# One forget-bias tile per head, held for a whole head pair

## The chip, the core and the metric

The kernel runs on one core of a Trainium2 chip. The metric is the device time of one execution in microseconds (us), as the median of several runs. Beside it there is one profiled execution: its instructions on five engines (PE is TensorE, DVE VectorE, ACT ScalarE, POOL GpSimd, SP SyncE, which here only issues DMAs), its DMA packets and the clock that TensorE was granted.

## What is computed

One layer of a streaming encoder, for a prompt of 1040 positions (16 meta tokens and 1024 frames) and a sample group of 32 positions with a cache of 272. One projection makes the queries, keys and values of two attention groups and a gate. The first group (4 heads, "differential") has a bias from the distance of query and key. The second (8 heads, "forgetting") has a bias that is a difference of running sums of log forget gates:

```
F = jnp.cumsum(LF, axis=1)
...
sf = jnp.einsum('bqhe,bkhe->bhqk', qf, Kf).astype(f32) * scale
sf = sf + (Fq_t[:, :, :, None] - Fk_t[:, :, None, :])
sf = jnp.where(kidx[None, :] <= qidx[:, None], sf, NEG)
pf = jax.nn.softmax(sf, axis=-1)
of = jnp.einsum('bhqk,bkhe->bqhe', pf.astype(Vf.dtype), Vf)
...
y = x + (out.astype(x.dtype) * jax.nn.silu(gate)) @ w_out_l
```

A term that is the same for all keys of a query falls out of the softmax. So the kernel needs, of `Fq - Fk`, only the part that runs over the keys, against any reference column.

## The kernel before

The work is cut into tasks, some thousand of them, each with an engine, a cost, a priority, dependencies and the buffers that it takes and gives back. A planner (`Graph.order`) walks through them in modelled time and writes out, for each engine, the order in which its instructions stand. The order is fixed when the program is built: on the chip each engine and the SP queue goes through its list in order, and waits on semaphores for its operands. So a task with another cost, another dependency or another buffer can move instructions on every engine behind it.

There are eight head pairs, `p` 0 to 7. Pairs 0 to 3 are the four differential heads, pairs 4 to 7 hold two forgetting heads each. A pair has its projections of v, k and q (line 827), its sample part, and its attention units. In a forgetting pair there are eight units, head by query group: `units = [(h, gg) for gg in range(4) for h in range(2)]` (line 1846). A query group has 256 queries, which are two blocks `i` of 128; block `i` attends to 144 + 128 i keys.

A block of a forgetting head goes through this chain: two matmuls a chunk of up to 512 keys into a score buffer `sc` and one that adds the mask (lines 1235 and 1237); a fused DVE pass that adds the bias tile `G`, scales and takes the minimum (line 1249); the exponential on ACT (1255); the reciprocal on DVE (1259); a split into two halves of 16 bits on ACT, POOL or DVE (1290 to 1323); a DMA transpose by SP (1335); and the products with the values on PE (1351, 1352, 1354), called the value products below. The planner places matmuls of projections (line 827, of later pairs or of the gate) between the scores of a block and its value products, and PE goes through them while the chain runs on the other engines.

The bias tile of a forgetting head comes to its unit in this way. `forget_tasks` has the running sum `F` of eight heads on eight partitions. Four DVE passes (line 1113) subtract, one for each query group, the value at the first query of the group, and four DMAs store the rows in the DRAM tensor `G_s` (line 1115). Before a pair begins, its 2 heads by 4 groups are loaded as eight rows (1177), multiplied by a scale of the pair on POOL (1180) and stored to `G_t` (1184). Then each unit has one DMA that spreads its row over 128 partitions (1192), as wide as the keys of its group: 272, 528, 784 or 1040 columns. The tile is one of the ring "G", which has two buffers (`RINGS`, line 247), so that a unit's tile can be fetched when the unit before the last one has read its own. The ring also serves the distance tile of the differential pairs and the two norm weights.

After the last pair the output projection (line 1770) runs by blocks of 128 rows, each of which needs the mixed values (`mix_s`) of all pairs and the gates (`gate_s`).

Of the kernel before, what the change touches and what calls it, by code (L numbers as in the profile page):

```python
# [9 lines left out]
F32 = mybir.dt.float32  # L10
# [4 lines left out]
ALU = mybir.AluOpType  # L15
# [6 lines left out]
NH = 8  # L22
# [67 lines left out]
class Graph:  # L90
# [9 lines left out]
    def add(self, eng, cost, fn, prio, deps=(), acq=(), use=(), move=0.0, spare=()):  # L100
        t = Task(eng, cost, fn, prio, deps, acq, use, move, spare)
        t.seq = len(self.tasks)
        self.tasks.append(t)
        return t
# [125 lines left out]
def tile_hymba(  # L230
# [72 lines left out]

    mix_s = dr.tile([1024, 1056], F32, tag="mix_s", name="mix_s")
    gate_s = dr.tile([1024, NT], F32, tag="gate_s", name="gate_s")
    G_s = dr.tile([NH, 4 * 1040], F32, tag="G_s", name="G_s")
    G_t = dr.tile([NH, 4 * 1040], F32, tag="G_t", name="G_t")
    Gs_s = dr.tile([NH, LS], F32, tag="Gs_s", name="Gs_s")
    mix_v = mix_s.rearrange("(k p) c -> p k c", p=128)
    gate_v = gate_s.rearrange("(k p) c -> p k c", p=128)  # L310
# [35 lines left out]
    def A(h, n, rows=128):  # L346
        assert h.ring == "arena" and n <= h.size
        return arena[:rows, h.at:h.at + n]
# [630 lines left out]
    def forget_tasks(prio):  # L979
# [123 lines left out]
                                          scalar1=F[:, c - 1:c], scalar2=None, op0=ALU.add)  # L1103
            carry = [add("dve", 800, fa, prio, [tm] + carry, [Fh] if part == 0 else [], [ph] + ([Fh] if part else []))]
        G_done = {}
        for gg in range(4):
            n = 1040
            gh = Hold("arena", n)

            def fg(gg=gg, n=n, gh=gh):  # L1110
                F = A(Fh, 1040, NH)
                b = 16 + 256 * gg
                dve.tensor_scalar(out=A(gh, n, NH), in0=F[:, :n], scalar1=F[:, b:b + 1], scalar2=None, op0=ALU.subtract)
            tg = add("dve", 65 + 0.6 * n, fg, prio, carry, [gh], [Fh])
            G_done[gg] = dma(lambda gg=gg, n=n, gh=gh: sp.dma_start(
                out=G_s[:, 1040 * gg:1040 * gg + n], in_=A(gh, n, NH)), prio, [tg], [], [gh])

        ph, FSh, GSh = Hold("pj"), Hold("arena", LS), Hold("arena", LS)

# [25 lines left out]
        w = -(-nk // n // 16) * 16  # L1145
        return [(i * w, min(nk, (i + 1) * w)) for i in range(n)]

    def bias_tasks(p, hd, gg, prio, G_done):

        h = Hold("G")  # L1150
        loc = {}
        if p < 4:
            sl = 2.0 ** (-2 * (p + 1))
            eh = Hold("arena", 1040)

            def f1():
                E = A(eh, 1040)
                pool.iota(E, pattern=[[-1, 1040]], base=912, channel_multiplier=1, allow_small_or_imprecise_dtypes=True)
                pool.tensor_scalar(out=E, in0=E, scalar1=Q[p]["inv"], scalar2=sl, op0=ALU.mult, op1=ALU.mult)

            def f2():
                E = A(eh, 1040)
                D = T([128, 1040], F32, "G", RINGS["G"])
                dve.scalar_tensor_tensor(out=D, in0=E, scalar=-1.0, in1=E, op0=ALU.mult, op1=ALU.max)
                loc["t"] = D
            t1 = add("pool", 2500, f1, prio, [cn.get("bias"), cn["gate"], Q[p]["t_tau"]], [eh, h], spare=[1088, 1088])
            t2 = add("dve", c_dve(1040), f2, prio, [t1], [], [eh, h])
            t3 = add("pool", 250, lambda: pool.memset(loc["t"][0:64, 976:1040], BIG), prio, [t2], [], [h])
            cn["bias"] = t3
            return loc, h, t3  # L1170
        n = 272 + 256 * gg
        if ("G", p) not in samp:
            gh = Hold("arena", 1040)
            a = 2 * (p - 4)

            def fl():
                sp.dma_start(out=A(gh, 1040, 8), in_=G_s[a:a + 2].rearrange("h (g n) -> (h g) n", g=4))

            def fm():
                pool.tensor_scalar(out=A(gh, 1040, 8), in0=A(gh, 1040, 8), scalar1=Q[p]["inv"][:8], scalar2=1.0,  # L1180
                                   op0=ALU.mult, op1=ALU.mult)

            def fo():
                sp.dma_start(out=G_t[a:a + 2].rearrange("h (g n) -> (h g) n", g=4), in_=A(gh, 1040, 8))
            t = dma(fl, prio - 50, [G_done[x] for x in range(4)] + [Q[p]["t_tau"]], [gh], kb=33)
            t = add("pool", 100 + 1.1 * 1040, fm, prio - 50, [t], [], [gh])
            samp["G", p] = dma(fo, prio - 50, [t], [], [gh], kb=33)

        def f():
            loc["t"] = T([128, 1040], F32, "G", RINGS["G"])  # L1190
            c = 1040 * (4 * hd + gg)
            sp.dma_start(out=loc["t"][:, :n], in_=G_t.rearrange("h n -> (h n)")[None, 8320 * (p - 4) + c:8320 * (p - 4) + c + n]
                         .broadcast_to([128, n]))
        cn["bias"] = dma(f, prio, [samp["G", p], cn["bias"]], [h], kb=n / 2)
        return loc, h, cn["bias"]

    mix_done = {}
# [645 lines left out]
    def pair_tasks(p):  # L1843
        base = 1000 + 100 * p
        sample_tasks(p, base + 3, G_done)
        units = [(0, gg) for gg in range(4)] if p < 4 else [(h, gg) for gg in range(4) for h in range(2)]
        av = {}
        dist = None
        for u, (hd, gg) in enumerate(units):
            if p >= 4 or u == 0:  # L1850
                dist = bias_tasks(p, hd, gg, base + u - 1, G_done)
            if hd == 0:
                av = {}
            unit_tasks(p, hd, gg, base + u, dist, av)

    done = -1
    for idx, (kind, p) in enumerate(order):
# [56 lines left out]
```

## Time and profile before

| what | us |
|---|---|
| median of 3 runs (881.67 to 883.38) | 882.83 |
| the profiled execution | 879.12 |
| its span | 877.4 |
| PE busy | 703.1 (80%) |
| DVE busy | 633.0 (72%) |
| ACT busy | 496.5 (57%) |
| POOL busy | 414.3 (47%) |
| packets of the DMA queue of SP, as a share of 16 engines | 60.4% |

The span is what the trace covers; the rest of the profiled execution's time lies around it. A busy time is a sum over stages with different limits, so that the table alone doesn't tell what a change is worth. In the order of time the stages are: the norm and the first projections with the forget gates (to about 134 us), mostly differential pairs (to about 420), the forgetting pairs (to about 740), the output projection (to the end).

### The profile page before, as it was taken

Reading aid. Unit: us, or ns where it says so; the run is one execution under the profiler, and the core shown is the slowest. Engines: PE = TensorE matmul, PEld = TensorE weight load, DVE = VectorE, ACT = ScalarE, POOL = GpSimd, SP = SyncE. Lnnn points to the kernel's source line nnn. Section 1 sums busy time; section 2 is a strip of 40 time slices with the busy share of each in tenths; the row PEclk is TensorE's granted clock in tenths of the full one; section 3 lists DMA queues with packets and bytes.
Section 4 is the critical chain, followed back from the end, with each engine's and each line's share of the span. In section 5 each row is a group of like instructions: output and inputs, shape, how many; then the busy total and the mean of one; then the engine's idle time right before and its main releaser. Section 6 shows DMA issues by size and latency. Waiting matters only on the chain. (4 is left out here: it accounts for less than half of the span.)

```text
span 877.4 us, 14974 instructions
## 1 busy us (share of the span) xinstructions
PE 703.1 (80%) x4967; PEld 456.3 (52%) x4967; DVE 633.0 (72%) x1672; ACT 496.5 (57%) x1136; POOL 414.3 (47%) x602
## 2 busy tenths in 40 slices
PE   4578887987876999899796978689788962888776
PEld 4455554665544576566564755356556542233333
DVE  5976587877766887988985857497797895454443
ACT  5843574666553776676675665377568752242222
POOL 2575233977556866866743654445452244200000
PEclk7679989999998999999998989799999985698899
DMA  8672426454423554554499688467959989753511
GB/s 248 122 147 62 93 54 88 106 94 103 95 65 74 127 102 98 115 117 115 105 194 182 127 168 163 111 144 167 208 123 204 277 204 243 232 173 121 153 63 49
DMA packets 240558, 119.27 MB, mean 136 GB/s; under 512 B 150569, under 2 KB 229745, under 8 KB 240481
## 3 DMA queue, kind: packets, MB, share of 16 engines
q1 hardware_dynamic: 240480, 118.32, 60.4%
q8 instruction: 39, 0.64, 0.3%
q14 instruction: 39, 0.31, 0.1%
HBM read 57.18 MB, written 22.07 MB: 90 GB/s over the span
## 5 line engine op out<-in xcount | busy, mean ns | idle before, releaser
L827 PE MATMUL pj<-hT,Whi 128*128 128x384 f16 (+4 forms) x1328 | 314.7, 321 | 2.0 <-DVE ge L938 1.5
L827 PE MATMUL pj<-hT,Wlo 128*128 128x416 f16 (+4 forms) x664 | 212.6, 320 | 4.4 <-DVE Wlo L648 4.4
L827 PEld LDWEIGHTS <-Whi 128*128 128x128 f16 x1328 | 133.3, 102 | 78.5 <-issue 11.5
L1249 DVE CUSTOM_DVE_ANT_0 arena<-sc,G,stats 128x400 f32<-128x400 f32 (+6 forms) x224 | 129.9, 590 | 43.3 <-PE sc L1235 22.4
L1255 ACT ACTIVATE arena<-arena,stats 128x144 f32<-128x144 f32 (+7 forms) x128 | 99.9, 780 | 38.8 <-DVE stats L1249 31.6
L1235 PE MATMUL sc<-k,q 128*128 128x400 f16 (+6 forms) x448 | 97.1, 317 | 29.4 <-DVE stats L1249 25.7
L583 POOL TENSOR_SCALAR diag<-ident,stats 128x128 bf16<-128x128 f32 x51 | 26.1, 513 | 154.9 <-ACT Wlo L1737 68.5
L827 PEld LDWEIGHTS <-Wlo 128*128 128x128 f16 x664 | 67.6, 102 | 38.1 <-DVE Wlo L648 4.7
L1351 PE MATMUL av<-arena,vn 128*128 128x128 f16 x288 | 43.9, 236 | 45.2 <-DMA arena<-arena 44.7
L1235 PEld LDWEIGHTS <-q 128*128 128x128 f16 x448 | 40.8, 101 | 57.6 <-issue 41.1
L627 ACT ACTIVATE Wlo<-raw 128x1024 bf16<-128x1024 f32 x27 | 28.5, 1055 | 63.8 <-DMA raw<-in_w_in_dram 63.8
L1770 PEld LDWEIGHTS <-Whi 128*128 128x128 f16 (+2 forms) x304 | 30.1, 102 | 58.7 <-issue 16.5
L827 PE MATMUL pj<-hT,Wghi 128*128 128x256 f16 (+2 forms) x240 | 58.2, 326 | 0.0
L1770 PE MATMUL pj<-arena,Whi 128*128 128x512 f16 (+4 forms) x152 | 49.7, 413 | 9.8 <-ACT Whi L1740 7.1
L1352 PEld LDWEIGHTS <-vn 128*128 128x128 f16 x288 | 30.7, 107 | 48.6 <-issue 47.6
L1290 POOL TENSOR_TENSOR arena<-arena 128x16 f16<-128x16 f32 (+7 forms) x56 | 46.5, 853 | 12.4 <-ACT arena L1284 12.1
L1306 DVE SCALAR_TENSOR_TENSOR arena<-arena,stats 128x128 f16<-128x128 f32 (+4 forms) x80 | 49.6, 663 | 2.6 <-ACT arena L1298 2.4
L1323 POOL TENSOR_TENSOR arena<-arena 128x16 f16<-128x16 f32 (+3 forms) x48 | 36.0, 773 | 25.8 <-ACT arena L1317 25.7
L1789 ACT ACTIVATE arena<-arena 128x512 bf16<-128x512 f32 (+3 forms) x19 | 11.5, 603 | 61.4 <-DVE arena L1784 61.4
L1352 PE MATMUL av<-arena,vn 128*128 128x128 f16 x288 | 44.3, 237 | 0.0
L1784 DVE SCALAR_TENSOR_TENSOR arena<-pj,stats,arena 128x512 f32<-128x512 f32 (+3 forms) x19 | 13.7, 721 | 42.3 <-PE pj L1770 38.9
L587 PE MATMUL tr<-diag,onesb 128*128 128x128 bf16 x51 | 11.7, 229 | 36.9 <-POOL diag L583 24.6
(310 smaller groups left out, 1786.7 us busy)
## 6 DMA issues: line engine op xcount, KB each, us to landing
raw<-in_w_in_dram SPq DMA_DIRECT2D x32, 512.0 KB, 7.5
arena<-in_x_prompt_dram SPq DMA_DIRECT2D x16, 512.0 KB, 9.7
raw<-in_w_out_dram SPq DMA_DIRECT2D x16, 512.0 KB, 4.6
k<-k SPq DMA_DIRECT2D x16, 268.0 KB, 3.4
G<-G_t SPq DMA_DIRECT2D x8, 520.0 KB, 4.7
mix_s<-mx SPq DMA_DIRECT2D x32, 128.0 KB, 3.4
arena<-mix_s SPq DMA_DIRECT2D x8, 512.0 KB, 6.3
arena<-gate_s SPq DMA_DIRECT2D x8, 512.0 KB, 6.0
```

The costliest lines, as they stand in the source:

```text
L583: pool.tensor_scalar(out=loc["d"], in0=ident, scalar1=col_, scalar2=1.0, op0=ALU.mult, op1=ALU.mult)
L627: ta = add("act", c_act(1024), lambda: act.activation(out=loc["lo"].bitcast(BF16), in_=loc["raw"], func=AF.Abs, accum_out=a), prio, [tl], ...
L827: mm(out, (W["hi"], W["hi"], W["lo"])[w][:, k, :], (hTh, hTl, hTh)[w][:, k, c0:c1], start=i == 0, stop=i == 23)
L1235: mm(s[:, :b - a], q, K[p]["t"][:, m, x, a:b], start=x == 0, stop=x == 1 and not mask)
L1249: dve.tensor_tensor_reduce(out=A(ph, nk)[:, a:b], in0=loc["s"][:, :b - a], in1=bl["t"][:, o + a:o + b], scale=Q[p]["tau"], scalar=3e38 if ...
L1255: te = add("act", c_act(nk) + 150, lambda ph=ph, nk=nk, mn=mn, sm=sm: act.activation(out=A(ph, nk), in_=A(ph, nk), func=AF.Exp, scale=-1.0 ...
L1290: (pool if on_pool else dve).tensor_tensor(out=A16(w, o, o + b - a), in0=x[:, a:b], in1=A16(w, h, h + b - a), op=ALU.subtract)
L1306: dve.scalar_tensor_tensor(out=A16(w, o, o + b - a), in0=x[:, a:b], scalar=rk, in1=A16(w, h, h + b - a), op0=ALU.mult, op1=ALU.subtract)
L1323: pool.tensor_tensor(out=A16(w, o, o + b - a), in0=x[:, a:b], in1=A16(w, h, h + b - a), op=ALU.subtract)
L1351: mm(out, vn[:, j, 128 * hd:128 * hd + 128], hi, start=j == 0, stop=False)
L1352: mm(out, vn[:, j, 128 * hd:128 * hd + 128], lw, start=False, stop=False)
L1770: mm(d, a, b, start=k == 0 and i == 0, stop=k == 7 and i == len(ops) - 1)
```

## The change

The bias of a forgetting head is made once for all four query groups. One DVE pass subtracts the value of `F` at column 528 in place of four that subtract the value at the first query of a group; one store in place of four fills `G_s`; the scale of a pair is applied to two rows in place of eight; and one broadcast of 1040 columns for each head takes the place of four of 272, 528, 784 and 1040. `pair_tasks` asks for a head's tile at its first unit (priorities `base - 1` and `base`) and hands the same tile to all four units, so that a pair holds both buffers of the ring until its heads are through.

```diff
--- before.py
+++ after.py
@@ -303,8 +303,8 @@
 
     mix_s = dr.tile([1024, 1056], F32, tag="mix_s", name="mix_s")
     gate_s = dr.tile([1024, NT], F32, tag="gate_s", name="gate_s")
-    G_s = dr.tile([NH, 4 * 1040], F32, tag="G_s", name="G_s")
-    G_t = dr.tile([NH, 4 * 1040], F32, tag="G_t", name="G_t")
+    G_s = dr.tile([NH, 1040], F32, tag="G_s", name="G_s")
+    G_t = dr.tile([NH, 1040], F32, tag="G_t", name="G_t")
     Gs_s = dr.tile([NH, LS], F32, tag="Gs_s", name="Gs_s")
     mix_v = mix_s.rearrange("(k p) c -> p k c", p=128)
     gate_v = gate_s.rearrange("(k p) c -> p k c", p=128)
@@ -1103,17 +1103,14 @@
                                           scalar1=F[:, c - 1:c], scalar2=None, op0=ALU.add)
             carry = [add("dve", 800, fa, prio, [tm] + carry, [Fh] if part == 0 else [], [ph] + ([Fh] if part else []))]
         G_done = {}
-        for gg in range(4):
-            n = 1040
-            gh = Hold("arena", n)
-
-            def fg(gg=gg, n=n, gh=gh):
-                F = A(Fh, 1040, NH)
-                b = 16 + 256 * gg
-                dve.tensor_scalar(out=A(gh, n, NH), in0=F[:, :n], scalar1=F[:, b:b + 1], scalar2=None, op0=ALU.subtract)
-            tg = add("dve", 65 + 0.6 * n, fg, prio, carry, [gh], [Fh])
-            G_done[gg] = dma(lambda gg=gg, n=n, gh=gh: sp.dma_start(
-                out=G_s[:, 1040 * gg:1040 * gg + n], in_=A(gh, n, NH)), prio, [tg], [], [gh])
+
+        gh = Hold("arena", 1040)
+
+        def fg():
+            F = A(Fh, 1040, NH)
+            dve.tensor_scalar(out=A(gh, 1040, NH), in0=F, scalar1=F[:, 528:529], scalar2=None, op0=ALU.subtract)
+        tg = add("dve", 65 + 0.6 * 1040, fg, prio, carry, [gh], [Fh])
+        G_done["p"] = dma(lambda: sp.dma_start(out=G_s, in_=A(gh, 1040, NH)), prio, [tg], [], [gh])
 
         ph, FSh, GSh = Hold("pj"), Hold("arena", LS), Hold("arena", LS)
 
@@ -1145,7 +1142,7 @@
         w = -(-nk // n // 16) * 16
         return [(i * w, min(nk, (i + 1) * w)) for i in range(n)]
 
-    def bias_tasks(p, hd, gg, prio, G_done):
+    def bias_tasks(p, hd, prio, G_done):
 
         h = Hold("G")
         loc = {}
@@ -1168,30 +1165,28 @@
             t3 = add("pool", 250, lambda: pool.memset(loc["t"][0:64, 976:1040], BIG), prio, [t2], [], [h])
             cn["bias"] = t3
             return loc, h, t3
-        n = 272 + 256 * gg
-        if ("G", p) not in samp:
+        if hd == 0:
             gh = Hold("arena", 1040)
             a = 2 * (p - 4)
 
             def fl():
-                sp.dma_start(out=A(gh, 1040, 8), in_=G_s[a:a + 2].rearrange("h (g n) -> (h g) n", g=4))
+                sp.dma_start(out=A(gh, 1040, 2), in_=G_s[a:a + 2])
 
             def fm():
-                pool.tensor_scalar(out=A(gh, 1040, 8), in0=A(gh, 1040, 8), scalar1=Q[p]["inv"][:8], scalar2=1.0,
+                pool.tensor_scalar(out=A(gh, 1040, 2), in0=A(gh, 1040, 2), scalar1=Q[p]["inv"][:2], scalar2=1.0,
                                    op0=ALU.mult, op1=ALU.mult)
 
             def fo():
-                sp.dma_start(out=G_t[a:a + 2].rearrange("h (g n) -> (h g) n", g=4), in_=A(gh, 1040, 8))
-            t = dma(fl, prio - 50, [G_done[x] for x in range(4)] + [Q[p]["t_tau"]], [gh], kb=33)
+                sp.dma_start(out=G_t[a:a + 2], in_=A(gh, 1040, 2))
+            t = dma(fl, prio - 50, [G_done["p"], Q[p]["t_tau"]], [gh], kb=8)
             t = add("pool", 100 + 1.1 * 1040, fm, prio - 50, [t], [], [gh])
-            samp["G", p] = dma(fo, prio - 50, [t], [], [gh], kb=33)
+            samp["G", p] = dma(fo, prio - 50, [t], [], [gh], kb=8)
+        c = 2 * (p - 4) + hd
 
         def f():
             loc["t"] = T([128, 1040], F32, "G", RINGS["G"])
-            c = 1040 * (4 * hd + gg)
-            sp.dma_start(out=loc["t"][:, :n], in_=G_t.rearrange("h n -> (h n)")[None, 8320 * (p - 4) + c:8320 * (p - 4) + c + n]
-                         .broadcast_to([128, n]))
-        cn["bias"] = dma(f, prio, [samp["G", p], cn["bias"]], [h], kb=n / 2)
+            sp.dma_start(out=loc["t"], in_=G_t[c:c + 1].broadcast_to([128, 1040]))
+        cn["bias"] = dma(f, prio, [samp["G", p], cn["bias"]], [h], kb=520)
         return loc, h, cn["bias"]
 
     mix_done = {}
@@ -1845,13 +1840,13 @@
         sample_tasks(p, base + 3, G_done)
         units = [(0, gg) for gg in range(4)] if p < 4 else [(h, gg) for gg in range(4) for h in range(2)]
         av = {}
-        dist = None
+        dist = {}
         for u, (hd, gg) in enumerate(units):
-            if p >= 4 or u == 0:
-                dist = bias_tasks(p, hd, gg, base + u - 1, G_done)
+            if hd not in dist:
+                dist[hd] = bias_tasks(p, hd, base + u - 1, G_done)
             if hd == 0:
                 av = {}
-            unit_tasks(p, hd, gg, base + u, dist, av)
+            unit_tasks(p, hd, gg, base + u, dist[hd], av)
 
     done = -1
     for idx, (kind, p) in enumerate(order):
```

The line numbers of the changed kernel are smaller by five from `bias_tasks` on: 1187 and below there answer to 1192 here. The planner's order moves on all five engines, from the forget gates on. Three places follow.

The first is the SP queue where pair 6 ends and pair 7 begins (`G<-G_t` is the spreading of a bias tile, `arena<-arena` the transpose of a block with 2 i + 3 tiles of 128, `raw` a weight load, `stg` rows of new keys on their way out, `ckr` and `cvr` cached keys and values). Before:

```order
L1192 DMA G<-G_t 128x272
L1335 DMA_TRANSPOSE arena<-arena 128x15x128
L793 DMA vm<-vm 16x256
L625 DMA raw<-in_w_in_dram 128x8x128
L1373 DMA mix_s<-mx 128x256
L1335 DMA_TRANSPOSE arena<-arena 128x17x128
L1192 DMA G<-G_t 128x272
L1457 DMA ckr<-in_cache_fox_k_dram 128x2x128
L1458 DMA ckr<-in_cache_fox_k_dram 16x128
L1192 DMA G<-G_t 128x528
L945 DMA gate_s<-ge 128x384
L1335 DMA_TRANSPOSE arena<-arena 128x15x128
```

The changed kernel, at the same place:

```order
L1188 DMA G<-G_t 128x1040
L1368 DMA mix_s<-mx 128x256
L1330 DMA_TRANSPOSE arena<-arena 128x15x128
L793 DMA vm<-vm 16x256
L625 DMA raw<-in_w_in_dram 128x8x128
L1330 DMA_TRANSPOSE arena<-arena 128x17x128
L1188 DMA G<-G_t 128x1040
L718 DMA out_dram<-stg 128x2x128
L721 DMA out_dram<-stg 16x128
L1330 DMA_TRANSPOSE arena<-arena 128x15x128
L1330 DMA_TRANSPOSE arena<-arena 128x17x128
```

The first broadcasts of a pair stand where they stood, among the transposes of the last blocks of the pair before, but are 1040 columns wide in place of 272; the later ones of 528, 784 and 1040 are gone from the list.

The second is PE near the end of pair 7, behind the scores of the largest block of head 0 (`q_7799` and `q_7754` are its queries, `vn` values, `Whi` and `Wlo` gate weights). Before:

```order
L1235 MATMUL sc<-k,q_7799 128x336
L1237 LDWEIGHTS identb
L1237 MATMUL sc<-mkb,identb 128x128
L1351 LDWEIGHTS vn
L1351 MATMUL av<-arena,vn 128x128
L1352 LDWEIGHTS vn
L1352 MATMUL av<-arena,vn 128x128
```

The changed kernel:

```order
L1230 MATMUL sc<-k,q_7754 128x336
L1232 LDWEIGHTS identb
L1232 MATMUL sc<-mkb,identb 128x128
L827 LDWEIGHTS Whi
L827 MATMUL pj<-hT,Whi 128x416
L827 LDWEIGHTS Wlo
L827 MATMUL pj<-hT,Wlo 128x416
L827 LDWEIGHTS Whi
L827 MATMUL pj<-hT,Whi 128x416
```

Matmuls of the gate projection, which were all used up before this point, now stand between these scores and the next value products: 32 of them lie between the scores of this block and its own value products, where there were none.

The third is no excerpt but a count over both lists. Between the last score matmul of a forgetting block and its value products there stood on average 126.6 matmuls on PE, and now 134.6; blocks with fewer than 45 projection matmuls in between were 14 of 64, and are 9 of 64. Single blocks move both ways: head 1, block 4 of pair 4 goes from 40 to 55, the same block of pair 5 from 39 to 47, head 0, block 6 of pair 6 from 120 to 88.

## Rows read from the trace of the kernel before

**Rows 1.** Windows by stage: stretch, PE, PEld, DVE, ACT, POOL busy, granted clock, DMA, GB/s
```profile
371.00:705.00 334.00, 280.33 (x2257) 195.63 (x2256) 258.20 (x741) 221.37 (x514) 163.71 (x265) 0.95 0.76 161
...
420.00:740.00 320.00, 253.34 (x2032) 177.32 (x2030) 242.03 (x689) 202.88 (x461) 146.84 (x229) 0.92 0.82 175
```

**Rows 2.** Waits of PE, 420 to 719 us: us in total, times, longest
```profile
PE av L1351 <- DMA arena<-arena: 33.5, 17, 8.7
PE sc L1235 <- DVE stats L1249: 10.9, 13, 3.0
```

**Rows 3.** Timeline of PE: start, us, operation, idle before and its releaser
```profile
440.02 0.34 PE L827 MATMUL pj<-hT,Whi 128*128 128x416 f16 x1
440.19 0.34 PE L827 MATMUL pj<-hT,Wlo 128*128 128x416 f16 x1
...
448.47 0.22 PE L1351 MATMUL av<-arena,vn 128*128 128x128 f16 x1 [1.33 <-DMA arena<-arena]
...
479.36 0.27 PE L1351 MATMUL av<-arena,vn 128*128 128x128 f16 x1 [6.62 <-DMA arena<-arena]
...
559.91 0.27 PE L1351 MATMUL av<-arena,vn 128*128 128x128 f16 x1 [8.72 <-DMA arena<-arena]
...
660.00 0.22 PE L1351 MATMUL av<-arena,vn 128*128 128x128 f16 x1 [4.34 <-DMA arena<-arena]
...
682.17 0.22 PE L1351 MATMUL av<-arena,vn 128*128 128x128 f16 x1 [0.32 <-DMA arena<-arena]
682.23 0.22 PE L1352 MATMUL av<-arena,vn 128*128 128x128 f16 x1
```

**Rows 4.** Timeline of the SP queue: start, us, what it issued
```profile
440.61 0.32 SPq L1192 DMA_DIRECT2D G<-G_t  x1
...
442.65 2.04 SPq L1335 DMA_TRANSPOSE arena<-arena  x1
...
466.75 0.53 SPq L1192 DMA_DIRECT2D G<-G_t  x1
467.33 0.63 SPq L625 DMA_DIRECT2D raw<-in_w_in_dram  x1
468.15 10.00 SPq L1335 DMA_TRANSPOSE arena<-arena  x2
...
677.42 0.52 SPq L1192 DMA_DIRECT2D G<-G_t  x1
678.11 1.20 SPq L1335 DMA_TRANSPOSE arena<-arena  x1
```

**Rows 5.** DMA queue of SP, and bias broadcasts by size: KB each, us to landing
```profile
q1 hardware_dynamic: 240480, 118.32, 60.4%
...
G<-G_t SPq DMA_DIRECT2D x8, 520.0 KB, 4.7
...
G<-G_t SPq DMA_DIRECT2D x8, 392.0 KB, 4.3
...
G<-G_t SPq DMA_DIRECT2D x8, 264.0 KB, 6.2
...
G<-G_t SPq DMA_DIRECT2D x8, 136.0 KB, 3.4
```

**Rows 6.** Line 1249, the reader of the bias: what its engine waited for
```profile
  PE sc L1235: 22.4, 20
  PE sc L1237: 13.3, 15
  DMA gs<-Gs_s: 1.6, 1
```

**Rows 7.** Lines 1192 and 1113: durations in ns, min, median, max
```profile
L1192 SPq DMA_DIRECT2D G<-G_t x32: 319/392/1590, 371.0 to 701.4; - x32
...
L1113 DVE TENSOR_SCALAR arena<-arena x4: 743/744/749, 133.7 to 135.7; 8x1040 f32<-8x1040 f32 x4
```

**Rows 8.** Waits of the SP queue: us in total, times, longest
```profile
SPq L1192 <- DVE stats L1249: 9.5, 9, 4.1
```

**Rows 9.** Second broadcast of pair 7 (SP) and its first reader (DVE), from timelines
```profile
658.47 0.38 SPq L1192 DMA_DIRECT2D G<-G_t  x1
...
663.59 0.37 DVE L1249 CUSTOM_DVE_ANT_0 arena<-sc,G,stats 128x144 f32<-128x144 f32 x1 [4.32 <-PE sc L1237]
```

**Rows 10.** The chain that ended last, in order of time
```profile
718.22 0.50 DVE arena L1249
...
731.20 5.05 DMA arena<-arena
...
746.87 9.96 PE pj L1770 x24
```

## The prediction

> **What bounds the kernel now.** I read the page by stages first. No engine is full in the stage that the change touches: from 420 to 740 us PE is busy for 253 of 320 us and DVE for 242, while the DMA engines have their highest share of any stage, 0.82 [rows 1]. So the next view is who PE waits for there. Nearly all of it is one kind: from 420 us to the last scores (719 us) PE stands at the first value product of a block and waits 33.5 us, in 17 waits, for the DMA transpose of the same block; the next kind, scores that wait for a free score buffer, has 10.9 us [rows 2]. The timeline shows the waits one by one, the longest at 559.91 and 479.36 us [rows 3]. The SP queue at the second of them shows why a transpose is late: a bias broadcast and a weight load go out at 466.75 and 467.33, and the two transposes behind them hold the queue for 10.00 us [rows 4].
>
> The chain that ended last goes from the last scores (the DVE pass at 718.22) over one transpose of 5.05 us into the output projection [rows 10], and everything behind is the same work in both kernels. The last scores come after the same PE work in both orders. So what the change is worth is what it does to the waits of PE before 719 us.
>
> The bias tile itself is not waited for: of the time that DVE stood before line 1249, all was for scores or other things, none for a `G` from `G_t` [rows 6]. The broadcasts matter through what they do to the DMA engines, to the SP queue and to the planner's order.
>
> **Part A, traffic.** The 32 broadcasts move 8 x (520 + 392 + 264 + 136) = 10,496 KB, the new eight 8 x 520 = 4,160 KB [rows 5]. That is 6,336 KB or 6.49 MB less. All packets of the queue took 60.4% of 877.4 us for 118.32 MB [rows 5], which is 530 us or 4.48 us for a MB, so the change takes away some 29 us of all 16 engines, out of 0.76 x 334 = 254 us that they are busy from 371 to 705 us [rows 1]: 11%.
> Most of this lies beside other work. Of the 17 waits, eight have a bias broadcast issued shortly before or during the flight of their transpose; the first is at 448.47 (broadcast at 440.61, transpose at 442.65), the last at 682.17 (677.42 and 678.11) [rows 3, 4]. Together they last 11.8 us. A broadcast can have cost a wait no more than its own time, 0.52 x 4.48 = 2.3 us for the widest, which cuts the 6.62 us at 479.36 to 2.3 and leaves 7.5 us as the upper end. The lower end is a loss, since the first two broadcasts of each pair grow by 384 KB, 1.7 us of all engines each, among the transposes of the largest blocks; that is the second rival below. I take a gain of 3 us, nearer to nothing than to the upper end, because the longest wait, 8.72 us, has no broadcast of the bias ahead of it.
> The trace prices a MB at 4.48 us in a mix that is mostly short packets. The Trainium skill gives the SBUF side of the DMA engines a ceiling of 435 GB/s (DMA: Bandwidth & Descriptors, Specifications). By that figure alone the traffic taken away would be an estimated 15 us, not 29, the most that the widest broadcast could have cost 1.2 us, and this part would be worth 2 us in place of 3. No row here shows a broadcast at that rate.
>
> **Part B, order.** The count at the end of the part on the change says that a block has on average 8 more matmuls between its scores and its value products. Their starts lie 0.17 us apart where they are 416 columns wide and 0.06 where they are value products [rows 3], so 8 of a mix are about 1 us of more cover. Taking at most 1 us from each of the 17 waits gives 13.6 us, which would be all if order did nothing else. It does: head 1, block 4 of pair 4, the one that waits 6.62 us, gains 15 projection matmuls (2.6 us), the same block of pair 5, with 8.72 us, gains 8 (1.4 us), but head 0, block 6 of pair 6, with 4.34 us at 660.00, loses 32 (5.4 us) [rows 3]. The planner puts value products where it believes that they are ready, so a longer cover also says that it sees the chain on DVE, ACT and POOL as longer. The ends are a gain of 26 us (all 33.5 us but what part A has taken) and a loss of 9 us (one more wait like the longest). I take 4 us, a third of the 13.6.
>
> **Part C, issue and DVE.** SP has 24 broadcasts less of 0.39 us, 9.4 us of queue in over 330, and it stood 9.5 us in nine waits for a tile that DVE had not given back [rows 7, 8]; with a tile that is held, six of eight such waits per pair fall away. Nothing but a transpose behind them makes that count, and those are in part A. Three DVE passes of 0.744 us go, at 133.7 to 136.4 us [rows 7]; nobody waits for them directly, and PE has projections there. The ends are 0 and 2.2 us, and I take 1, since DVE is what gives score and projection buffers back. The scale on POOL has as many instructions as before, on two partitions in place of eight.
>
> **Sum.** 3 + 4 + 1 = 8 us. From the profiled execution's 879.1 us this gives 871; the median of the runs lies 3.7 us above that execution, so the forecast for the median is 882.8 - 8 = **874.8 us**, 0.9% faster.
>
> **Rivals.** *Hidden anyway.* No engine waits for the bias, the transfers were fetched one unit ahead, and the waits of PE would form again at other blocks, since the planner aims its value products at the same readiness as before. For it speaks that nothing on DVE waited for `G_t` [rows 6] and that the longest wait has no broadcast ahead. Against it speaks a DMA share of 0.82 with late transposes [rows 1, 4]. Time: within 1.7 us of 882.8.
> The Trainium skill states this as a rule: a DMA that is issued early, with its semaphore waited on late, has its fixed cost overlapped (DMA: Bandwidth & Descriptors, Rules for kernel authors). By that rule the kernel would keep its 882.8; the trace agrees as to waits, none of them for `G_t`, and leaves open what the bytes cost others.
>
> *Slower at the start of a pair.* A pair's first two tiles are now 520 KB in place of 136 KB, they can only be fetched when the last two units of the pair before have been read, and they go out among the transposes of its largest blocks. The second one has the least room: in pair 7 it is issued at 658.47 and read at 663.59, 5.1 us later [rows 9], and 520 KB land in 4.7 us in the median, 136 KB in 3.4 [rows 5]. If each of the eight makes DVE and the transposes behind it wait for its additional 384 KB, 1.3 us (the difference of the medians) to 1.7 us (by 4.48 us a MB), that is 10 to 14 us; less the 4 us of parts A and C that stay, 6 to 10 us: 889 to 893. It decides from the point where the landing takes longer than those 5.1 us. Against it: the planner knows the larger transfer and has moved the first scores of head 1 back behind more of head 0. An order that happens to be worse (the loss of 9 us in part B) would come out at the same time.
>
> *Much faster.* If more cover and less traffic meet, most of the 33.5 us go: 20 us, 863. For it speaks that short covers (under 45 projection matmuls) fall from 14 blocks to 9, and that TensorE had a mean granted clock of 0.92 in the stage [rows 1], which would rise with fewer stalls. Against it: block 6 of pair 6 and the other scatter of part B.
>
> That only some of the broadcasts go is no rival: the order of the changed kernel holds eight.
>
> **How the numbers follow.** Forecast, 866 to 880: 0.43. Much faster, 858 to 866: 0.14. Hidden, 881.1 to 884.6: 0.16. Slower, 885 to 893 and a little above: 0.27. The range from 861 to 890 leaves out about a third of the much faster case, a fifth of the slower one and little more, so that it holds some 0.8. By the same cases, and with 0.2% (1.7 us, about what a measurement of this kernel can tell from no change) as the bound: faster 0.57, same 0.16, slower 0.27.
>
> **What would show it.** Part A: the DMA share from 420 to 740 us falls by some 8 hundredths, the queue's 118.3 MB to 111.8, and waits with a broadcast ahead are gone. Part B: the sum of PE's waits at line 1346 (1351 before) for transposes up to the last scores falls from 33.5 us to about 25, and the last scores come at about 711 us. Part C: one pass in place of four behind the running sums. The second rival would show as idle time of DVE before line 1244 (1249 before) that ends with a `G<-G_t` landing, at the starts of pairs 4 to 7. What would make the prediction wrong without either: a shift before 420 us, in the differential pairs, whose order moves too from about 134 us on and for which the trace of before gives no sign.

## The result and the profile after

The changed kernel takes 870.51 us in the median of four runs (868.61 to 875.07), the kernel before, on the same chip, 883.11 us (four runs, 881.67 to 883.97). The ratio, worked out from all runs and not from the two medians (0.9857), is 0.9865 with a 95% interval from 0.9831 to 0.9899: 1.35%, or 11.9 us of 882.8. The forecast was 874.8 us, a gain of 8 us. The sign is right and the range holds the time; the gain is half as large again as forecast, and the experiments show that it does not come from the parts that the forecast gave most to.

The profiled execution of the changed kernel is the slowest of its four (875.07 us, span 873.4 us), that of the kernel before lies under its median (879.12 us, span 877.4 us). The two are 4.0 us apart, so that the traces of this pair hold a third of the gain. Its stages and its queue, which answer to [rows 1, 5] (stretch; PE, PEld, DVE, ACT and POOL busy; granted clock; DMA share; GB/s):

```profile
134.00:420.00 286.00, 244.77 (x1790) 167.28 (x1788) 217.95 (x586) 174.93 (x423) 191.54 (x260) 0.93 0.50 98
420.00:740.00 320.00, 260.42 (x2090) 180.85 (x2089) 251.36 (x707) 207.02 (x473) 160.30 (x239) 0.93 0.73 156
...
q1 hardware_dynamic: 236880, 111.53, 58.0%
```

From 420 to 740 us the DMA share went from 0.82 to 0.73 and PE is busy for 260 us in place of 253. The waits of PE from 420 us to the last scores (716.3 us here), which answer to [rows 2] (us in total, times, longest):

```profile
PE av L1346 <- DMA arena<-arena: 23.7, 12, 6.5
PE sc L1230 <- DVE stats L1244: 10.7, 19, 2.0
```

The waits for transposes are 9.8 us less; those for score buffers stayed. On the timeline of PE, which answers to [rows 3]:

```profile
480.12 0.26 PE L1346 MATMUL av<-arena,vn 128*128 128x128 f16 x1 [3.87 <-DMA arena<-arena]
...
562.57 0.27 PE L1346 MATMUL av<-arena,vn 128*128 128x128 f16 x1 [6.49 <-DMA arena<-arena]
...
648.65 0.22 PE L1346 MATMUL av<-arena,vn 128*128 128x128 f16 x1 [0.43 <-DMA arena<-arena]
655.58 0.22 PE L1346 MATMUL av<-arena,vn 128*128 128x128 f16 x1 [2.83 <-DMA arena<-arena]
```

Head 1, block 4 of pair 5 is at 562.57 and still waits 6.49 us (8.72 before). Head 1, block 4 of pair 4, which waited 6.62 us, no longer waits; the 3.87 us are another block of that pair. Head 0, block 6 of pair 6, from whose cover the new order takes 32 matmuls, is at 648.65: it waits 0.43 us in place of 4.34.

The bias tile itself (the eight broadcasts; what the reader's engine waited for; issue to landing; a piece of the chain that ended last), which answers to [rows 6, 7, 10]:

```profile
L1188 SPq DMA_DIRECT2D G<-G_t x8: 326/527/1130, 363.3 to 653.6; - x8
...
  DMA G<-G_t: 0.8, 1
...
DMA to landing us min/median/max: 3.5/3.7/3.8
...
653.57 4.62 DMA G<-G_t
...
730.13 4.49 DMA arena<-arena
743.18 10.05 PE pj L1765 x24
```

DVE waits once, for 0.8 us, for a tile, at the start of pair 7. Behind the first matmul of the output projection (743.18 us, 746.87 before) both kernels take 130 us.

Before 420 us there is something new. The waits of PE from 134 to 420 us, of the changed kernel:

```profile
PE av L1342 <- DMA arena<-arena: 14.8, 6, 7.7
...
PE sc L1230 <- DVE stats L1244: 4.9, 9, 0.8
```

and of the kernel before:

```profile
PE sc L1235 <- DVE stats L1249: 13.5, 14, 2.9
...
PE tr L587 <- ACT stg L712: 6.3, 2, 5.9
...
PE av L1347 <- DMA arena<-arena: 1.8, 2, 1.1
```

In the new order the value products of the differential pairs wait 14.8 us for transposes, where they waited 1.8 us. In all PE stands still little longer there, 286 - 244.77 = 41.2 us against 39.4 before, since other waits went. What differs as well is the granted clock, 0.93 above and 0.96 in the kernel before:

```profile
134.00:420.00 286.00, 246.65 (x1852) 166.99 (x1851) 226.91 (x609) 179.83 (x433) 196.44 (x270) 0.96 0.49 99
```

### The profile page after: what moved, and what is told of

The parts are those of the page before. It is cut to its first block, busy times and chain, and to the rows that moved or that the text cites. A ratio compares the mean times of both kernels' runs of the same rounds, so it can differ in the third digit from the quotient of the medians.

```text
span 873.4 us, 14882 instructions
## 1 busy us (share of the span) xinstructions
PE 709.9 (81%) x4967; PEld 460.6 (53%) x4967; DVE 631.3 (72%) x1669; ACT 495.2 (57%) x1136; POOL 420.3 (48%) x602
## 3 DMA queue, kind: packets, MB, share of 16 engines
q1 hardware_dynamic: 236880, 111.53, 58.0%
## 5 line engine op out<-in xcount | busy, mean ns | idle before, releaser
L1244 DVE CUSTOM_DVE_ANT_0 arena<-sc,G,stats 128x400 f32<-128x400 f32 (+7 forms) x224 | 129.7, 590 | 42.1 <-PE sc L1230 20.0
L1230 PE MATMUL sc<-k,q 128*128 128x400 f16 (+7 forms) x448 | 99.1, 319 | 20.3 <-DVE stats L1244 16.9
L1346 PE MATMUL av<-arena,vn 128*128 128x128 f16 x288 | 42.8, 233 | 36.3 <-DMA arena<-arena 36.2
L1347 PEld LDWEIGHTS <-vn 128*128 128x128 f16 x288 | 30.1, 105 | 34.9 <-issue 33.5
L1779 DVE SCALAR_TENSOR_TENSOR arena<-pj,stats,arena 128x512 f32<-128x512 f32 (+3 forms) x19 | 13.7, 721 | 44.7 <-PE pj L1765 39.4
L1318 POOL TENSOR_TENSOR arena<-arena 128x16 f16<-128x16 f32 (+3 forms) x48 | 39.0, 833 | 14.3 <-ACT arena L1312 14.1
L1347 PE MATMUL av<-arena,vn 128*128 128x128 f16 x288 | 43.0, 234 | 0.0
L1342 PE MATMUL av<-arena,vn 128*128 128x128 f16 x144 | 28.7, 233 | 15.9 <-DMA arena<-arena 14.8
```

Source lines behind the costliest of these rows:

```text
L1230: mm(s[:, :b - a], q, K[p]["t"][:, m, x, a:b], start=x == 0, stop=x == 1 and not mask)
L1244: dve.tensor_tensor_reduce(out=A(ph, nk)[:, a:b], in0=loc["s"][:, :b - a], in1=bl["t"][:, o + a:o + b], scale=Q[p]["tau"], scalar=3e38 if ...
L1318: pool.tensor_tensor(out=A16(w, o, o + b - a), in0=x[:, a:b], in1=A16(w, h, h + b - a), op=ALU.subtract)
L1342: mm(out, vn[:, j, 0:128], hi, start=j == 0, stop=False)
L1346: mm(out, vn[:, j, 128 * hd:128 * hd + 128], hi, start=j == 0, stop=False)
L1347: mm(out, vn[:, j, 128 * hd:128 * hd + 128], lw, start=False, stop=False)
```

## The experiments

Theory 1 is the prediction: traffic 3 us, order 4 us, issue and DVE passes 1 us. Theory 2: the gain is the new order, one draw among many. Theory 3: the gain is the dropped work, whatever the order. Where theory 3 led, theories 4 and 5 part it into bytes and places in SP's queue. All ratios are to the kernel before, timed on the same chip; a difference of two ratios has the root of the sum of both squared half widths as its own half width.

### The change without its order

Both kernels keep the planner's tasks of before; those that are dropped emit nothing. On PE, ACT, DVE and POOL the same instructions stand in the same order as before, but for the three DVE passes and the sizes of the scale. The first kernel has the one pass, one store and two-row scale of the change and all 32 broadcasts; the second also holds the tile:

```
-                dve.tensor_scalar(... scalar1=F[:, b:b + 1] ...)
+                if gg:
+                    return
+                dve.tensor_scalar(... scalar1=F[:, 528:529] ...)
...
         def f():
+            if gg:
+                loc["t"] = held[p, hd]
+                return
+            loc["t"] = held[p, hd] = T([128, 1040], F32, "G", RINGS["G"])
```

> The order of before on every engine (the planner's tasks are kept), with the changed kernel's arithmetic on the bias: one DVE pass at column 528 and one store in place of four, the scale on two partitions in place of eight; all 32 broadcasts stay, each in its old place and width. It differs from before only in part C without the issue of broadcasts. Theory 1 (traffic and order together): 0 to 1 us under before, ratio 0.999 to 1.000. Theory 2 (the gain is the new order): 1.000. Theory 3 (the gain is the traffic): 1.000. If it is more than 2 us faster, the passes and small transfers were mis-sized.

> As the run with all 32 broadcasts in the order of before, but with eight: the first broadcast of each head is 1040 columns wide and its tile is held, the 24 others are left out of the queue and nothing takes their place. All of the change but its order. Theory 1: parts A and C without part B, 4 us under before, ratio 0.995, and the waits of PE for transposes up to the last scores fall from 33.5 to about 29 us. Theory 2 (order alone): ratio 1.000, waits 33 us. Theory 3 (traffic alone): as the changed kernel, 0.986, waits 24 us. If the first tiles of a pair, wider by 384 KB, make DVE wait at the starts of pairs, it is 6 to 10 us slower than by theory 1, and DVE has idle time that ends with a landing of a bias tile.

> The run e4_oldplan_8 again, beside three others in the order of before that differ from it in one thing each. All theories: 0.987, as before (0.9839 to 0.9899).

With 32 broadcasts: 878.29 us, ratio 0.9967 (0.9933 to 1.0), 2.9 us where no theory gave more than 1, but with an interval that reaches to no change. With eight: 869.9 us, 0.9869 (0.9839 to 0.9899), and again on another chip 873.07 us, 0.9872 (0.9838 to 0.9906). The kernel with eight has the changed kernel's 0.9865 without its order. Theory 2 falls, and with it half of theory 1. The waits of PE for transposes up to the last scores, of the two in this sequence:

```profile
PE av L1351 <- DMA arena<-arena: 31.7, 17, 7.9
```

```profile
PE av L1354 <- DMA arena<-arena: 26.2, 11, 9.2
...
420.00:740.00 320.00, 256.97 (x2042) 180.37 (x2040) 248.86 (x703) 204.09 (x465) 151.96 (x233) 0.90 0.70 157
```

The same PE order waits 5.5 us less where 24 broadcasts are gone. The two first output projections are at 747.2 and 742.1 us.

### Other orders of the same work

```
-MARGIN = 1.1
+MARGIN = 1.09
```

in the kernel before, in the kernel above with eight broadcasts, and in the changed kernel.

> The kernel before with one number of its planner changed (the factor on its estimates of durations, 1.10 to 1.09), which has nothing to do with the bias: same work, same bytes, another order from the start of the differential pairs on (4344 of 9253 rows of PE move, the change itself moves 4662). Theory 1 (order counts through the cover of transposes): within 4 us of before either way, ratio 0.995 to 1.005. Theory 2 (the result of the change is one draw from the scatter of re-planning): anything within 1.4 per cent of before, and a ratio under 0.99 would alone carry it. Theory 3 (traffic): 1.000.

> The eight broadcasts in the order of r_before_margin (same rows on PE, ACT; the 24 broadcasts and three DVE passes gone), which had 0.9939 with all 32. Theory 3 (traffic and passes, whatever the order): the same 11 to 12 us again, 0.981, which would be the fastest kernel so far. Theory 1 (traffic 3 us, the rest order): 0.990. Theory 2: 0.994.

> The changed kernel with the same number of its planner changed (1.10 to 1.09): same work and bytes as the changed kernel, another order (4618 rows of PE move). Theory 3 (the traffic makes the gain, an order is a draw): between 0.981 and 0.992. Theory 1 (this order has more cover than others): slower than the changed kernel's 0.9865, up to 0.995.

| tiles and order of tasks | factor 1.10 | factor 1.09 |
|---|---|---|
| 32 broadcasts, as before | 1 | 0.9939 (0.9912 to 0.9965) |
| eight broadcasts, tasks as before | 0.9869, 0.9872 | 0.9788 (0.9759 to 0.9818) |
| eight broadcasts, changed kernel | 0.9865 | 0.9797 (0.9771 to 0.9823) |

Down a column, the work that the change drops is worth 1.3 and 1.5% (0.0130 and 0.0151 +- 0.0040 between the first two rows), and the order that comes with it nothing that shows (0.9870 and 0.9865; 0.9788 and 0.9797, each within its interval). Along a row, a number that has nothing to do with the bias gives 0.6 to 0.8% in all three. So order does count, by as much as a whole term of the sum; the order that this change brought was not measurably better. The two kernels at 1.09 are the fastest of this study (863.08 and 863.91 us). Why that plan is better was not followed up. The runs at 1.09 list a higher granted clock, 0.919, 0.924 and 0.917 in the mean down the column, against 0.911, 0.912 and 0.914 at 1.10; whether that is a cause or goes with fewer stalls isn't settled.

### Bytes, or places in SP's queue

Two kernels put something back where the 24 broadcasts were, in the order of before with eight held tiles. One sends 8 columns to a tile that nobody reads, the other the old width to a scratch area in DRAM:

```
             if gg:
                 loc["t"] = held[p, hd]
+                x = T([128, 8], F32, "Gx", 1)
+                sp.dma_start(out=x, in_=G_t[c:c + 1, 0:8].broadcast_to([128, 8]))
                 return
```

```
             if gg:
                 loc["t"] = held[p, hd]
+                sp.dma_start(out=G_x[8 * gg + c - 8, :, 0:n], in_=G_t[c:c + 1, 0:n].broadcast_to([128, n]))
                 return
```

> The order of before with eight broadcasts (the run e4_oldplan_8), and in the place of each of the 24 that are gone a broadcast of 8 columns (4 KB) into a tile that nobody reads: SP issues as many transfers as in before at the same places, without their bytes and without their wait for a tile that DVE gives back. e4_oldplan_8 had 0.9869, all 32 broadcasts in the same order 0.9967. Theory 4 (the 8.6 us between the two are bytes, or the wait for the tile): as e4_oldplan_8, 0.987. Theory 5 (they are the queue: 24 issues of 0.39 us ahead of transposes): 0.997, or in between by 24 x 0.39 = 9.4 us at most.

> The order of before with eight broadcasts, and in the place of each of the 24 that are gone one of its old width that writes to a scratch area in DRAM that nobody reads: the queue's bytes and issues of before without the wait of SP for a tile that DVE gives back (8.6 us in seven waits in the run with 32). Theory 4a (bytes): 0.997, and the DMA share from 420 to 740 us goes from 0.70 back to 0.81. Theory 4b (the wait of SP for a tile, with the transposes queued behind it): 0.987, as e4_oldplan_8. A write to DRAM may be dearer or cheaper than one to SBUF; the DMA share tells.

The small transfers give 876.26 us, 0.9937 (0.9915 to 0.9958): 24 x 4 KB take back 0.0067 +- 0.0031, 5.9 us of the gain (3.1 to 8.6). The wide ones give 884.59 us, 1.004 (1.0017 to 1.0063): 9.54 MB more than the small ones for 9.1 +- 2.8 us, at a DMA share of 0.82 from 420 to 740 us. The 24 wide ones wait for no tile (4.3 us in two waits of SP stay, at the eight that do fill one), and yet the kernel is slower than the one with 32 broadcasts: the wait for a tile alone is not what the broadcasts cost (theory 4b, 0.987, falls). That it costs nothing isn't shown, because this kernel also moves 3.1 MB more than the one with 32 (121.17 MB against 118.02), its first broadcasts being wide too, and writes the 24 to DRAM. Part of the cost is bytes and part is the place in the queue; neither theory 4 nor theory 5 holds alone.

Two more tell the parts apart by other means: the same 4 KB transfers issued by ACT, and 32 broadcasts of which each is 1040 wide:

```
-                sp.dma_start(out=x, in_=G_t[c:c + 1, 0:8].broadcast_to([128, 8]))
+                act.dma_start(out=x, in_=G_t[c:c + 1, 0:8].broadcast_to([128, 8]))
```

```
-            sp.dma_start(out=loc["t"][:, :n], in_=G_t[c:c + 1, 0:n].broadcast_to([128, n]))
+            sp.dma_start(out=loc["t"], in_=G_t[c:c + 1, 0:1040].broadcast_to([128, 1040]))
```

> The run e7_issue_only (0.9937) with its 24 transfers of 4 KB issued by ACT in place of SP, at the same places of the program: the same transfers on the same 16 engines, but not in SP's queue ahead of the transposes. Theory 5a (what these small transfers cost is the place in SP's queue): as e4_second, 0.987. Theory 5b (it is the transfers themselves): 0.994. ACT pays for 24 issues; if that is what counts, its scores' passes come later and the ratio goes above 0.994.

> The run e6_oldplan_32 (0.9967) with every one of its 32 broadcasts 1040 columns wide: same issues, same waits for a tile, 6.5 MB more (the amount that the change takes away, added). Theory 4 (bytes, at one price): as much slower as 6.5 MB made e4_oldplan_8 faster, 1.006. Theory 4c (a MB costs more the fuller the DMA engines are, which had 0.81 in the stage): more than that, 1.010 to 1.020. Theory 5 (issues alone): 0.997.

From ACT: 870.64 us, 0.9858 (0.9818 to 0.9899). That is the ratio with no such transfers at all, and 0.0079 +- 0.0046 under the same transfers on SP, 7.0 us (2.9 to 11.0). Theory 5a: what they cost is their place in SP's queue. All 32 wide: 885.16 us, 1.0017 (0.9993 to 1.0042), 0.0050 +- 0.0042 over the kernel with 32 of the old widths: 6.3 MB more for 4.4 us (0.8 to 8.1), so that bytes cost something too. It is under theory 4's 1.006, whose price for a MB had the issues in it, and at a DMA share of 0.85 in the stage it leaves no room for theory 4c, from 1.010.

What a place in the queue does to the transposes behind it is seen where the small transfers come from SP (line 1195; ns min, median, max; then SP's timeline, two transposes in one row):

```profile
L1195 SPq DMA_DIRECT2D Gx<-G_t x24: 325/432/1547, 427.0 to 697.7; - x24
...
506.65 0.34 SPq L945 DMA_DIRECT2D gate_s<-ge  x1
507.09 0.37 SPq L1195 DMA_DIRECT2D Gx<-G_t  x1
507.56 4.08 SPq L1340 DMA_TRANSPOSE arena<-arena  x2
```

and where they come from ACT:

```profile
L1195 ACTq DMA_DIRECT2D Gx<-G_t x24: 326/327/354, 426.5 to 691.5; - x24
...
504.96 0.36 SPq L945 DMA_DIRECT2D gate_s<-ge  x1
505.42 3.50 SPq L1340 DMA_TRANSPOSE arena<-arena  x2
```

From the start of the gate transfer to the end of the two transposes' issue there are 4.99 us with a small transfer in between and 3.96 without: 0.45 for the place, and 0.58 because the transposes behind it hold SP longer. On SP the issue of 4 KB takes up to 1.55 us, as that of the wide ones does [rows 7]; ACT is never held for more than 0.35 us. No single wait of PE carries the difference: up to the last scores it waits 28.0 us for transposes, 12.4 for score buffers and 3.8 at line 587 with the small transfers on SP, and 26.5, 10.8 and 2.7 us with them on ACT. Over the whole span even these differences are made up elsewhere. PE with the small transfers on SP (span 874.6 us) and on ACT (span 866.5 us):

```profile
PE 708.0 (81%) x4967; PEld 459.1 (52%) x4967; DVE 631.1 (72%) x1669; ACT 496.2 (57%) x1136; POOL 414.7 (47%) x602
...
PE 700.8 (81%) x4967; PEld 455.8 (53%) x4967; DVE 632.1 (73%) x1669; ACT 496.4 (57%) x1136; POOL 415.2 (48%) x602
```

PE stands still for 166.6 and 165.7 us; what differs between these two executions is how long it takes over the same matmuls, at a granted clock of 0.903 and 0.916 (0.910 and 0.913 in the mean over all runs of the two). So the times show that a place in SP's queue costs something, and one piece of the timeline how it delays a transpose; how that reaches the end of the kernel, by waits or by the clock, is open.

How bytes cost is seen best at a wait that the prediction did not have, that of PE at line 587 behind a weight load. SP, ACT and PE of the kernel before:

```profile
512.39 0.60 SPq L625 DMA_DIRECT2D raw<-in_w_in_dram  x1
...
516.29 1.23 SPq L1192 DMA_DIRECT2D G<-G_t  x1
...
521.21 1.06 ACT L627 ACTIVATE Wlo<-raw 128x1024 bf16<-128x1024 f32 x1 [4.44 <-DMA raw<-in_w_in_dram]
...
522.88 0.27 PE L587 MATMUL tr<-diag,onesb 128*128 128x128 bf16 x1 [4.08 <-POOL diag L583]
```

with eight broadcasts, in the same order:

```profile
514.45 0.60 SPq L625 DMA_DIRECT2D raw<-in_w_in_dram  x1
...
521.71 1.06 ACT L627 ACTIVATE Wlo<-raw 128x1024 bf16<-128x1024 f32 x1 [2.25 <-DMA raw<-in_w_in_dram]
...
523.39 0.22 PE L587 MATMUL tr<-diag,onesb 128*128 128x128 bf16 x1 [1.51 <-POOL diag L583]
```

and with the small transfers in the queue:

```profile
512.32 0.59 SPq L625 DMA_DIRECT2D raw<-in_w_in_dram  x1
...
519.84 1.06 ACT L627 ACTIVATE Wlo<-raw 128x1024 bf16<-128x1024 f32 x1 [3.58 <-DMA raw<-in_w_in_dram]
```

From the issue of the weight load to ACT's work on it there are 8.82 us with a broadcast issued behind it, 7.26 without and 7.52 with 4 KB in its place. The other kernels in this order agree: 9.19 and 9.46 us in two with 32 broadcasts, 8.05 where a wide one goes to DRAM, 7.12 to 7.41 in three with none there from SP. So the load is late where a broadcast goes out 3.9 us behind it, and PE's wait falls from 4.08 to 1.51 us without it.

### The broadcasts that are left

```
         def f():
-            loc["t"] = T([128, 1040], F32, "G", RINGS["G"])
+            if p > 4:
+                loc["t"] = held[hd]
+                return
+            loc["t"] = held[hd] = T([128, 1040], F32, "G", RINGS["G"])
```

in the changed kernel, and the same in the order of before.

> The changed kernel, in its own order, with two of its eight broadcasts: those of pair 4; pairs 5 to 7 read these two tiles again (their bias is not computed rightly, which changes values and no instruction on PE, DVE, ACT or POOL). It takes another 3.1 MB away, some 14 us of all 16 engines, all at the starts of pairs. Theory 1: at part A's price of 3 us for 6.49 MB, 1.4 us under the changed kernel, ratio to before 0.985. Theory 2: the same as the changed kernel, 0.9865. Theory 3: at 12.6 us for 6.49 MB, 6 us under the changed kernel, 0.979. If the wide tiles at the starts of pairs cost what the second rival charged (10 to 14 us for eight), 8 to 10 us, 0.976.

> The run e4_oldplan_8 with two broadcasts in place of eight: those of pair 4; pairs 5 to 7 read these tiles again (their bias is not computed rightly). 3.1 MB less, at the starts of pairs, in the order of before. Theory 4 (bytes, at one price of 1.3 us for a MB): 4 us under e4_second, ratio 0.982. Theory 4c (a MB costs nothing any more where the DMA engines are at 0.70): as e4_second, 0.987, as it was in the order of the changed kernel, where the same step gave 0.9894 against 0.9865.

873.03 us, 0.9894 (0.9861 to 0.9927), and 869.89 us, 0.9834 (0.9794 to 0.9874). Against their kernels with eight broadcasts that is 0.0029 +- 0.0047 slower and 0.0036 +- 0.0046 faster. Leaving out six more broadcasts brings nothing that both orders show; the 4 us of one price for a MB are not excluded by the second alone. What they would cost if the second rival held, 8 to 10 us, is.

## Why the prediction was right, and where it was not

| part | forecast, us (ends) | measured, us |
|---|---|---|
| A, bytes and the wait for the tile | 3 (a loss to 7.5) | 2.6 (-0.9 to 6.2): 32 broadcasts against 24 small ones and eight |
| B, order | 4 (-9 to 26) | 0.4 (-3.2 to 4.0): changed kernel against eight in the order of before |
| C, issues | with the passes 1 (0 to 2.2) | 5.9 (3.1 to 8.6) and, by way of ACT, 7.0 (2.9 to 11.0) |
| C, passes and stores | in the 1 above | 2.9 (0 to 5.9), not told from nothing |
| sum | 8 | 11.8; the change itself 11.9 (8.9 to 14.9) |

The measured rows are steps between neighbouring kernels, from the one before to the changed one, so that their sum meets the change by construction. That the forecast of 8 us came as near as it did is in part luck: part B was put 3.6 us too high and part C 7.8 us too low.

**Part A** has the right size, within an interval that reaches from a loss to twice the forecast; by the prices of 0.7 to 1.0 us for a MB that the wide transfers give (4.4 us for 6.3 MB, 9.1 us for 9.54 MB), the 6.49 MB would be an estimated 4.5 to 6 us. Its mechanism was too narrow: it charged bytes with delays of transposes alone, and the largest single wait that went in the order of before belongs to a weight load (4.08 to 1.51 us). Those 2.57 us are also more than the bound by row, 2.3 us for a wait. The prediction passed over this wait when it called nearly all of PE's waiting one kind: the transposes are 33.5 of 52.9 us in that view, which also has, of the kernel before,

```profile
PE tr L587 <- POOL diag L583: 4.7, 2, 4.1
```

The longest wait, for block 4 of pair 5, has no broadcast ahead, as the prediction said: it is 8.72 us before and 9.25 us with the 24 gone.

**Part C** is the step that failed. It says that only a transpose behind them makes SP's 9.4 us of issues count, "and those are in part A". Part A then priced bytes, and the issues were priced nowhere. A transfer of 4 KB costs as much in SP's queue as a wide one, since an issue there holds SP for 0.43 us in the median and up to 1.55 us, and the transposes behind it start later. The 24 issues were 9.4 us of SP by the rows, from the median; the mean is higher (the 24 small ones held SP for 14.3 us in sum, 0.60 us each). By the two differences of times 5.9 and 7.0 us reached the end of the kernel, with lower ends of 3.1 and 2.9, and not the 1 us that was taken. The upper end of 2.2 us came from the DVE passes and left the queue out, though [rows 4, 8] showed SP held for 10.00 us by two transposes and waiting 9.5 us for tiles. (These were nine waits in all; "six of eight such waits per pair" counts broadcasts.)

The Trainium skill says that starting transfers from several engines saves only the time to start them, which is usually small beside the transfer (DMA: Bandwidth & Descriptors, Issuing engines are not separate DMA queues). The rows agree on each transfer, 0.43 us of issue against 3.2 us to land. What the saving can be worth is seen here: taking 24 such starts off SP gave 7.0 us (2.9 to 11.0), where transposes stand behind them in the queue.

**Part B** was drawn from the one stage that the argument looked at. There it came about as forecast: 23.7 us of waits where the order of before with the same traffic has 26.2 and 27.6, and block 4 of pair 4 waits no more, block 6 of pair 6 for 0.43 us. What ate it is what the prediction named as its blind spot, a shift in the differential pairs. PE reaches the first mask matmul of pair 4 (418.4 us, 419.4 before) with 65 matmuls less behind it, an estimated 7 us of work (from 420 to 740 us it is busy for 260.42 us in place of 253.34). Standing still explains 1.8 us of that: the transposes there make PE wait 14.8 us in place of 1.8, but other waits went. The rest goes with the granted clock from 134 to 420 us, 0.93 in place of 0.96, which on some 245 us of work is an estimated 7 to 8 us. It is no accident of one execution: the changed order with two broadcasts has 0.94 there, the nine kernels in the order of before have 0.95 or 0.96. Whether the lower clock comes from where the waits now fall was not tried. The longest of the waits:

```profile
268.69 0.58 SPq L625 DMA_DIRECT2D raw<-in_w_in_dram  x1
269.38 10.71 SPq L1330 DMA_TRANSPOSE arena<-arena  x1
...
282.16 0.27 PE L1342 MATMUL av<-arena,vn 128*128 128x128 f16 x1 [7.69 <-DMA arena<-arena]
```

A forecast of 4 us still lies at the edge of the interval; that the order is worth nothing is near the middle of it, at both factors. The count of matmuls between scores and value products was no guide for single blocks: the one that lost 32 waits 0.43 us in place of 4.34.

**Rivals.** *Hidden anyway* argued that a transfer for which nobody waits is free. Nobody waited for the 24, and with their issues they cost 8.5 us (4.9 to 12.1). *Slower at the start of a pair*: its sign, DVE idle until a `G<-G_t` lands, came to 0.8 us in one place, and six of the eight can be left out for nothing that shows. The wide tile landed in 3.7 us in the median, under the 5.1 us from which this rival would decide; but in the order of before, with eight, it landed in 7.4 us and DVE did not wait for it either, so that the landing time by itself does not decide. *Much faster* did not come: 870.5 us lies in the forecast's own 866 to 880. Nor did fewer stalls raise the granted clock from 420 to 740 us: it is 0.92 before, 0.93 in the changed kernel and 0.90 with eight broadcasts in the order of before.

**Signs.** DMA share 0.82 to 0.73 (forecast: 0.08 less), queue 111.53 MB (111.8), waits for transposes 23.7 us (25). Last scores at 716.3 us, where 711 were forecast; this execution is 4.6 us above its median.

## What to carry to other kernels

Price every DMA that a change removes twice: its bytes on the engines, and its place in the issuing queue ahead of what somebody waits for; the second does not shrink with the bytes, and here the two were of one size as far as their intervals tell. Before costing a new order by the stage that the change aims at, read what it moves in the other stages, their waits and their granted clock; one unrelated step of the planner moved this kernel by 0.6 to 0.8%, so the parts of a change should be timed in the old order before a gain is put down to order. Where one queue carries both transposes and bulk loads, taking small transfers to another engine's queue is worth a try.

## What the runs showed of the hardware

The issue of a DMA on SP takes no less for 4 KB than for 136 to 520 KB (432 and 392 ns in the median, 1.55 and 1.59 us at most), and 0.33 to 0.35 us on ACT, whose queue holds nothing else in that kernel.

The longest waits that are left in the changed kernel stand behind weight loads and not behind the bias. A transpose issued 0.7 us after a load of 512 KB held SP for 10.71 us (269.38), at a DMA share of 0.29 from 255 to 285 us; in the same order with two broadcasts it is 10.71 us again. The wait of 6.49 us at 562.57 stands behind a load at 549.42 and a transpose that held SP for 6.93 us at 550.23. Whether the load or the transpose itself holds the queue there was not tried.
